# Attention scores as three f32r passes in a hybrid decoder block

## The chip, the cores and the metric

The kernel runs on one core of one Trainium2 chip. The metric is the device time of one execution in microseconds; runs of the kernel before took 970.04 to 971.68 us, with a median of 970.68 us over three runs. Everything is float32 data; products on TensorE are made either as float32 or as f32r, the chip's reduced float32 format, with values that were split into a high and a low part.

## The reference

A decoder block of one layer on 512 tokens of width 1024. Two branches share one input projection: a gated delta rule (8 heads of 128, in chunks) and a forgetting attention (8 heads of 128). Their outputs are merged by gates, and a squared-ReLU MLP of width 4096 follows. The part that the change touches is the attention:

```python
fqh = rmsnorm(to_heads(fq, FOX_HEADS), fox_q_norm_g[l])
fkh = rmsnorm(to_heads(fk, FOX_HEADS), fox_k_norm_g[l])
...
for i in range(t // FOX_BLOCK):            # 4 blocks of 128 queries
    q0 = i * FOX_BLOCK; q1 = q0 + FOX_BLOCK
    s = (einsum('bhqd,bhkd->bhqk', q[:, :, q0:q1], k[:, :, :q1]) * scale
         + cum[:, :, q0:q1, None] - cum[:, :, None, :q1])
    p = softmax(where(mask, s, -inf), axis=-1)
    outs.append(einsum('bhqk,bhkd->bhqd', p, v[:, :, :q1]))
```

So a head has four score products: 128 queries against 128, 256, 384 and 512 keys.

## The kernel before, in words

**Stages.** The kernel first normalises x and makes its high and low parts (`uhi`, `ulo`; to about 55 us). Then come the projections of the recurrence, `w_z` and `w_gdn`, by `dense` (L284): for each unit of weights, 8 contraction blocks with three f32r products of 512 columns (L290, L291, L294). The attention's q, k, v, the gates and later the projection of the attention's output come from `stream` (L959). It works by a scheme that replaces eight block products by seven (P1 to P7), with f32r products of 256 columns (L993), 24 for each unit. The merge (`w_pg`, by `dense`), `w_o` and the MLP (`w_u`, `w_d`; L1218 in the profile) end the kernel from about 609 us on.

**Weights.** Each weight tile arrives by DMA (`load`, L209), is copied to its high part by ScalarE (L271) and has its low part subtracted by VectorE (L272), two units ahead of the product (`prefetch_split`). In the MLP the same steps are L1462 and L1469.

**Side work.** Work that isn't the main sequence of weight products is written as Python generators, `tasks`. Each unit of the main sequence calls `tick()`, which lets every task go on to its next `yield`; I call that a round. The recurrence's heads (`head`), its inversion (`invert`, small VectorE steps L690 and L692), its scan over chunks and the attention (`fox_worker`) are such tasks. What a task writes in a round stands there in the program's order. The tile framework then plans: it simulates the program with its own estimates of durations and may reorder instructions on an engine; only the MLP's are in part kept in the order written.

**The attention.** Two `fox_worker` tasks take heads from the list `fq`, where `stream` puts each head once its q and k are there. A worker, per head: squares and a reciprocal root for the norms (L892 to L898), two empty rounds, then four transposes each of q and k into two PSUM banks `ptq` and `ptk` (L907, L908), copied to `qT` and `kT` by ScalarE with a scale (L911, L912). After a round, in each of six rounds, a stage of three query blocks: bias rows by ScalarE (L925, L926), the score product (L928), the sum with the bias and the row's extreme by VectorE (L931), the exponential by ScalarE (L933); one round later the reciprocal and the scaling (L940, L941) and the transposes of the probabilities (L944, copied in L946); one round later the product with v (L953). The head's output is copied (L956) and stored. While the second group of the recurrence is projected, `hold` keeps the workers from taking a further head.

**Buffers.** 53 pages of 128x512 float32 (`page`) are shared by nearly all of these; a page is free again when its last reader is done. Five PSUM banks with the tag "at" (`atps`) serve transposes, scores, scans and the rest; three serve the main sequence. ScalarE's functions stand in tables that have to be loaded (ACT_TABLE_LOAD): the exponential of L933, the sigmoid of L1095 and the SiLU of L611 and L1062 are not in one table here, as the loads in the profile show.

**After the attention.** `outputs_in` (L1091) waits until the recurrence, the workers and their stores are done and `stream` has begun its chunk 6; it applies the sigmoids to the gates (L1095) and splits the recurrence's outputs (rows read in L555, split in L301, L302). These feed the `w_pg` products of the merge.

Of the kernel before, what the change touches and what calls it, by code (L numbers as in the profile page):

```python
# [7 lines left out]
F32 = mybir.dt.float32  # L8
F32R = mybir.dt.float32r
AF = mybir.ActivationFunctionType  # L10
ALU = mybir.AluOpType
# [4 lines left out]
P = 128  # L16
# [28 lines left out]
def hybrid_block(tc, a, out):  # L45
# [21 lines left out]
    def nm(s):  # L67
        n_names[0] += 1
        return f"{s}_{n_names[0]}"
# [5 lines left out]
    def page(dt=F32, s="pg"):  # L75
        if s in FOX_TAGS:
            return fxp.tile([P, T], dt, tag=s, name=nm(s))
        tag = TAGS_OF.get(s, s)
        if tag in TAGS:
            return pgp.tile([P, T], dt, tag=tag, name=nm(s), bufs=TAGS[tag])  # L80
        return pgp.tile([P, T], dt, tag="pg", name=nm(s))
# [3 lines left out]
    def const(shape, s, dt=F32):  # L85
        return (cp if s in KEEP else cm).tile(shape, dt, tag=s, name=s)

    def small(n, s="sm"):
        return smp.tile([P, n], F32, tag="sm", name=nm(s))
# [12 lines left out]
    def atps(s="at"):  # L102
        return pat.tile([P, T], F32, tag="at", name=nm(s))

    def v3(ap, n):
        return ap.rearrange("p (a b) -> p a b", a=n)

    def bc(ap, n):
        return ap.unsqueeze(2).to_broadcast(list(ap.shape) + [n])

    def cs(c):
        return slice(c * P, (c + 1) * P)

    mm = nc.tensor.matmul
    vec, act, pool = nc.vector, nc.scalar, nc.gpsimd
# [23 lines left out]
    def start(gen):  # L139
        tasks.append(gen)  # L140
        return gen
# [3 lines left out]
    def store_late(dst, src):  # L145

        for _ in range(LATE):
            yield
        nc.sync.dma_start(dst, src)
# [172 lines left out]
    def small_in(name, shape, eng=None):  # L322
        t = const(shape, "c_" + name)
        (eng or nc.sync).dma_start(t, a[name])
        return t
# [19 lines left out]
    fk_g = small_in("fox_k_norm_g", [P, 1])  # L345
# [10 lines left out]
    fqs = const([P, 1], "fqs")  # L356
    pool.tensor_scalar(fqs, fq_g, float(P) ** -0.5, None, op0=ALU.mult)

    def rsq(dst, src):
        pool.tensor_tensor(dst, src, expo[:, 0:src.shape[-1]], op=ALU.pow)  # L360
# [501 lines left out]
    fq = []  # L862
# [6 lines left out]
    def bias_rows(n):  # L869

        if n < len(fq) and n not in rows_of:
            rows_of[n] = row_page(3, fq[n][0])
        return rows_of.get(n)

    def fox_worker(after=None):

        while after is not None and not inverted[after]:
            yield
        while taken[0] < H:
            if taken[0] >= len(fq) or hold[0]:  # L880
                yield
                continue
            h, qk, vt = fq[taken[0]]
            nr = bias_rows(taken[0])
            taken[0] += 1
            nd = page(s="nd")
            pool.affine_select(out=v3(nd[:, :], NCH), in_=v3(nr[:, :], NCH), compare_op=ALU.is_ge, fill=-1e30, base=0,
                               pattern=[[0, NCH], [-1, P]], channel_multiplier=1)
            sq = small(16, "fss")
            for half in range(2):  # L890
                junk = page(s="junk")
                act.activation(junk, qk[half], AF.Square)  # L892
                vec.tensor_reduce(sq[:, 4 * half:4 * half + 4], v3(junk[:, :], 4), axis=AX.X, op=ALU.add)
            vec.tensor_scalar(sq[:, 0:8], sq[:, 0:8], 1.0 / P, EPS, op0=ALU.mult, op1=ALU.add)
            rsq(sq[:, 8:16], sq[:, 0:8])
            for half in range(2):
                t = v3(qk[half][:, :], 4)
                pool.tensor_tensor(t, t, bc(sq[:, 8 + 4 * half:12 + 4 * half], P), op=ALU.mult)  # L898
            yield
            yield  # L900
            bias_rows(taken[0])
            ptq = atps("fqT")
            ptk = atps("fkT")
            for tb in range(NCH):
                t = qk[tb // 2]
                i = tb % 2
                nc.tensor.transpose(ptq[:, cs(tb)], t[:, cs(2 * i)], ident)  # L907
                nc.tensor.transpose(ptk[:, cs(tb)], t[:, cs(2 * i + 1)], ident)  # L908
            qT = page(s="fq")
            kT = page(s="fk")  # L910
            act.activation(qT, ptq, AF.Copy, scale=fqs)  # L911
            act.activation(kT, ptk, AF.Copy, scale=fk_g)  # L912
            yield
            while not vt:
                yield
            po = None
            st = {}
            for step in range(NCH + 2):
                i = step
                if i < NCH:  # L920
                    n = (i + 1) * P
                    s = cs(i)
                    bias = page(s="bias")
                    if i:
                        act.activation(bias[:, :n - P], nr[:, :n - P], AF.Identity, bias=cc[:, i, h:h + 1])  # L925
                    act.activation(bias[:, s], nd[:, s], AF.Identity, bias=cc[:, i, h:h + 1])  # L926
                    psc = atps("sc")
                    mm(psc[:, :n], qT[:, s], kT[:, :n], start=True, stop=True)  # L928
                    sm = small(4, "fsm")
                    pt = page(s="p")  # L930
                    vec.tensor_tensor_reduce(out=pt[:, :n], in0=psc[:, :n], in1=bias[:, :n], scale=-1.0,  # L931
                                             scalar=3.0e38, op0=ALU.add, op1=ALU.min, accum_out=sm[:, 0:1])
                    act.activation(pt[:, :n], pt[:, :n], AF.Exp, bias=sm[:, 0:1], scale=-1.0,  # L933
                                   accum_out=sm[:, 1:2])
                    st[i] = [pt, sm]
                i = step - 1
                if 0 <= i < NCH:
                    n = (i + 1) * P
                    pt, sm = st[i]
                    vec.reciprocal(sm[:, 2:3], sm[:, 1:2])  # L940
                    vec.tensor_scalar(pt[:, :n], pt[:, :n], sm[:, 2:3], None, op0=ALU.mult)  # L941
                    pT = atps("pT")
                    for c in range(i + 1):
                        nc.tensor.transpose(pT[:, cs(c)], pt[:, cs(c)], ident)  # L944
                    pTs = page(s="pTs")
                    act.copy(pTs[:, :n], pT[:, :n])  # L946
                    st[i] = pTs
                i = step - 2
                if 0 <= i < NCH:
                    if po is None:  # L950
                        po = atps("fo")
                    for c in range(i + 1):
                        mm(po[:, cs(i)], vt[c], st[i][:, cs(c)], start=(c == 0), stop=(c == i))  # L953
                yield
            o = page(s="ob")
            act.copy(o, po)  # L956
            stores.append(start(store_late(obd[:, h].rearrange("i p t -> p i t"), v3(o[:, :], 2))))
# [110 lines left out]
    box = {}  # L1068
    start(decays(0, box, gt))
    fws = [start(fox_worker()) for _ in range(NFW)]  # L1070
    fu = []
    ch0 = gdn_group(0, box, {1: lambda: fu.append(start(factors_u()))})
# [377 lines left out]
    for k, (w, c, p, s_) in enumerate(MLP):  # L1450
# [6 lines left out]
        n = pos[0]  # L1457
        pos[0] += 1
        new = range(len(units), min(len(seq), n + 1 + LA_MLP))
        for m in new:  # L1460
            hi, lo = whl.tile([P, D], F32R, tag="hi", name=nm("hi")), whl.tile([P, D], F32R, tag="lo", name=nm("lo"))
# [5 lines left out]
        for m in new:  # L1467
            hi, lo = units[m]
# [108 lines left out]
```

## Time and profile before

| | |
|---|---|
| median of 3 runs | 970.68 us (970.04 to 971.68) |
| profiled execution | 970.2 us, span 968.4 us |
| TensorE busy (PE) | 957.4 us, 99% |
| weight loads (PEld) | 868.9 us, 90% |
| VectorE busy (DVE) | 743.1 us, 77% |
| ScalarE busy (ACT) | 646.4 us, 67% |
| GpSimd busy (POOL) | 217.4 us, 22% |
| granted TensorE clock | 1.000 of full speed |

How to read it: the span is the time from the first to the last instruction. A matmul's end is modelled, and matmuls overlap, so PE at 99% says that TensorE nearly always had work in flight and not that each instruction was as short as it could be. PEld is the loading of the stationary operand, which runs beside the products. "Idle before" in a group's row is the idle time of that engine just ahead of its instructions, with the instruction that ended it. The chain that ended last is followed back from the last instruction; its pieces are start and length in microseconds, engine, tile and line.

### The profile page before, as it was taken

To read this page: it belongs to the slowest core of one execution; us is meant where nothing else is said; L and a number is where in the kernel's file an instruction comes from. 1 tells how busy PE (TensorE), PEld (TensorE's weight loads), DVE (VectorE), ACT (ScalarE), POOL (GpSimd) and SP (SyncE) were. 2 spreads that over 40 slices of the span, in tenths; PEclk is the share of its full clock that TensorE was granted. 3 is DMA by queue.
4 is the path that set the end of the run, shared out by engine and by line. 5 is a ranking of instruction groups with operands and counts; after the bars stand their busy time and mean duration, and the time that the engine had idled before them with its cause. 6 is when DMAs were issued, how large, how long until landed. Compare 5 with 4: busy or idle time off the path is not lost.

```text
span 968.4 us, 17456 instructions
## 1 busy us (share of the span) xinstructions
PE 957.4 (99%) x6610; PEld 868.9 (90%) x6610; DVE 743.1 (77%) x1249; ACT 646.4 (67%) x1096; POOL 217.4 (22%) x224
## 2 busy tenths in 40 slices
PE   9999999999999999999999999999999999999998
PEld 6788889998888999989999899889989989988986
DVE  6877979956478799665656887979886796697696
ACT  7879755778575767889556454678755755666761
POOL 1503222340343243322220110202122021121110
PEclk9999999999999999999999999999999999999999
DMA  8457679755677877657689687878798788888883
GB/s 288 138 156 240 187 181 204 170 147 165 207 235 185 195 179 150 153 143 195 189 178 319 153 221 204 156 184 171 173 213 180 197 165 202 182 176 197 191 168 113
DMA packets 87291, 180.38 MB, mean 186 GB/s; under 512 B 8152, under 2 KB 41048, under 8 KB 87208
## 3 DMA queue, kind: packets, MB, share of 16 engines
q0 software_dynamic: 17392, 63.12, 37.6%
q1 hardware_dynamic: 69816, 116.15, 37.4%
q8 instruction: 52, 0.85, 0.3%
q14 instruction: 31, 0.25, 0.1%
HBM read 160.11 MB, written 19.14 MB: 185 GB/s over the span
## 4 chain that ended last, share of the span: by engine, by line
PE 93%; ACT 4%; DVE 1%; issue 1%; DMA 1%; SPq 0%; ACTq 0%; DVEq 0%
PE mlp L1218 36%; PE st L993 23%; PE mm L294 7%; PE mm L290 7%; PE mm L291 7%; PE fo L953 2%; PE sc L928 2%; PE pT L944 1%; PE v L804 1%; PE kk L649 1%; PE kq L657 1%; PE o L825 1%; PE o L824 1%; ACT hi L271 1%; DMA x<-xT 1%
## 5 line engine op out<-in xcount | busy, mean ns | idle before, releaser
L1462 ACT CAST hi<-draw 128x1024 fp32r<-128x1024 f32 x124 | 129.9, 1049 | 116.8 <-PE mlp L1218 101.2
L1469 DVE TENSOR_TENSOR lo<-draw,hi 128x1024 fp32r<-128x1024 f32 x124 | 151.3, 1222 | 45.9 <-ACT hi L1462 42.7
L271 ACT CAST hi<-sraw 128x1024 fp32r<-128x1024 f32 x84 | 87.9, 1048 | 83.9 <-PE st L993 49.0
L272 DVE TENSOR_TENSOR lo<-sraw,hi 128x1024 fp32r<-128x1024 f32 x84 | 105.5, 1257 | 26.1 <-ACT hi L271 20.9
L1218 PE MATMUL mlp<-hi,shi 128*128 128x512 f32 x280 | 109.4, 391 | 0.7 <-ACT hi L1462 0.6
L1218 PE MATMUL mlp<-hi,slo 128*128 128x512 f32 x280 | 109.1, 390 | 0.0
L1218 PE MATMUL mlp<-lo,shi 128*128 128x512 f32 x280 | 109.0, 389 | 0.0
L1218 PE MATMUL mlp<-shi,hi 128*128 128x256 f32 x448 | 90.3, 283 | 0.0
L1218 PE MATMUL mlp<-slo,hi 128*128 128x256 f32 x448 | 90.3, 283 | 0.0
L1218 PE MATMUL mlp<-shi,lo 128*128 128x256 f32 x448 | 90.3, 283 | 0.0
L291 PE MATMUL mm<-ulo,hi 128*128 128x512 f32 x216 | 84.8, 395 | 1.3 <-DVE ulo L305 1.3
L290 PE MATMUL mm<-uhi,hi 128*128 128x512 f32 x216 | 84.8, 396 | 0.1
L232 POOL DMA_DIRECT2D sraw<-w_st x36 | 31.6, 878 | 190.1 <-DVE lo L272 141.2
L993 PE MATMUL st<-lo,hi 128*128 128x256 f32 x432 | 73.9, 287 | 0.0
L993 PE MATMUL st<-hi,lo 128*128 128x256 f32 x432 | 72.2, 285 | 0.0
L993 PE MATMUL st<-hi,hi 128*128 128x256 f32 x432 | 71.7, 287 | 0.0
L1218 PEld LDWEIGHTS mlp<-shi,hi 128*128 128x128 f32 x448 | 70.6, 192 | 0.9
L1218 PEld LDWEIGHTS mlp<-shi,lo 128*128 128x128 f32 x448 | 69.9, 192 | 0.0
L1218 PEld LDWEIGHTS mlp<-slo,hi 128*128 128x128 f32 x448 | 69.8, 192 | 0.0
L272 DVE TENSOR_TENSOR lo<-raw,hi 128x1024 fp32r<-128x1024 f32 (+1 forms) x42 | 50.1, 1197 | 22.0 <-ACT hi L271 16.1
L1218 PEld LDWEIGHTS mlp<-hi,shi 128*128 128x128 f32 x280 | 52.6, 188 | 11.9 <-ACT hi L1462 0.8
L1218 PEld LDWEIGHTS mlp<-lo,shi 128*128 128x128 f32 x280 | 52.6, 188 | 11.0
(343 smaller groups left out, 2314.2 us busy)
## 6 DMA issues: line engine op xcount, KB each, us to landing
sraw<-w_st POOLq DMA_DIRECT2D x36, 512.0 KB, 6.1
draw<-w_u POOLq DMA_DIRECT2D x32, 512.0 KB, 6.1
draw<-w_d POOLq DMA_DIRECT2D x32, 512.0 KB, 6.9
sraw<-w_st SPq DMA_DIRECT2D x27, 512.0 KB, 5.1
draw<-w_d SPq DMA_DIRECT2D x26, 512.0 KB, 4.4
raw<-w_gdn SPq DMA_DIRECT2D x24, 512.0 KB, 4.0
draw<-w_u SPq DMA_DIRECT2D x24, 512.0 KB, 4.5
hd<-hd SPq DMA_DIRECT2D x34, 256.0 KB, 4.1
```

The lines of the kernel that those rows point to most:

```text
L232: nc.gpsimd.dma_start(raw, a[w][c, q, s_], accum_op=ALU.add)
L271: act.copy(hi[:, c], raw[:, c])
L272: vec.tensor_tensor(lo[:, c], raw[:, c], hi[:, c].bitcast(F32), op=ALU.subtract)
L290: mm(o, w, rhi(k), start=(k == 0), stop=False)
L291: mm(o, w, rlo(k), start=False, stop=False)
L294: mm(o, lo[:, k * cols:(k + 1) * cols], rhi(k), start=False, stop=(k == KT - 1))
L928: mm(psc[:, :n], qT[:, s], kT[:, :n], start=True, stop=True)
L953: mm(po[:, cs(i)], vt[c], st[i][:, cs(c)], start=(c == 0), stop=(c == i))
L993: mm(o, u, w, start=first and t == 0 and k == 0 and j == 0 and x is hi, stop=x is lo and k == 3, skip_group_check=True)
L1218: return (lambda *args, **kw: tc.keep_in_program_order(f(*args, **kw))) if self.pinned[0] else f
L1462: pact.copy(hi, raws[m][0])
L1469: pvec.tensor_tensor(lo, raws[m][0], hi[:, :].bitcast(F32), op=ALU.subtract)
```

## The change

The transposed q and k of a head are written as f32r high parts (`qT`, `kT`, by ScalarE as before), and VectorE makes f32r low parts (`ql`, `kl`) by scaling the transposes once more and subtracting the high parts. The score products of query blocks 1, 2 and 3 (256, 384 and 512 keys) become three f32r passes that add up in PSUM: high by high, high q by low k, low q by high k. Block 0 (128 keys) keeps a float32 product; its operands are made by VectorE in a further page, `qk0`. A further `yield` stands before the scores.

```diff
-            qT = page(s="fq")
-            kT = page(s="fk")
+            qk0 = page(s="qk0")
+            qT, ql, kT, kl = [page(F32R, "fqk") for _ in range(4)]
             act.activation(qT, ptq, AF.Copy, scale=fqs)
             act.activation(kT, ptk, AF.Copy, scale=fk_g)
+            for x, src, by in ((qk0[:, 0:P], ptq, fqs), (qk0[:, P:2 * P], ptk, fk_g)):
+                vec.tensor_scalar(x, src[:, 0:P], by, None, op0=ALU.mult)
+            for hi, lo, src, by in ((qT, ql, ptq, fqs), (kT, kl, ptk, fk_g)):
+                vec.scalar_tensor_tensor(lo, src, by, hi[:, :].bitcast(F32), op0=ALU.mult, op1=ALU.subtract)
+            yield
             yield
             while not vt:
                 yield
...
                     psc = atps("sc")
-                    mm(psc[:, :n], qT[:, s], kT[:, :n], start=True, stop=True)
+                    if i:
+                        mm(psc[:, :n], qT[:, s], kT[:, :n], start=True, stop=False)
+                        mm(psc[:, :n], qT[:, s], kl[:, :n], start=False, stop=False)
+                        mm(psc[:, :n], ql[:, s], kT[:, :n], start=False, stop=True)
+                    else:
+                        mm(psc[:, :n], qk0[:, 0:P], qk0[:, P:2 * P], start=True, stop=True)
```

## The prediction, made before the changed kernel ran

> **What bounds the kernel now.** I read the page's totals, then the chain that ended last, then the busy time by stretches, then the single groups.
>
> ```profile
> span 968.4 us, 17456 instructions
> PE 957.4 (99%) x6610; PEld 868.9 (90%) x6610; DVE 743.1 (77%) x1249; ACT 646.4 (67%) x1096; POOL 217.4 (22%) x224
> PE 93%; ACT 4%; DVE 1%; issue 1%; DMA 1%; SPq 0%; ACTq 0%; DVEq 0%
> PE mlp L1218 36%; PE st L993 23%; PE mm L294 7%; PE mm L290 7%; PE mm L291 7%; PE fo L953 2%; PE sc L928 2%; PE pT L944 1%; PE v L804 1%; PE kk L649 1%; PE kq L657 1%; PE o L825 1%; PE o L824 1%; ACT hi L271 1%; DMA x<-xT 1%
> ```
>
> TensorE carries 93% of the chain, and the scores of L928 stand in it with 2%. Matmul durations overlap, so I take the price of a product from the chain, where a piece lasts until the next one starts. By stretches (columns: length, then busy time and count for PE, PEld, DVE, ACT, POOL):
>
> ```profile
> 140.00:360.00 220.00, 220.00 (x1724) 202.61 (x1723) 166.71 (x367) 153.10 (x310) 68.29 (x64) 1.00 0.73 187
> 360.00:395.00 35.00, 35.00 (x287) 34.10 (x286) 34.14 (x86) 24.41 (x45) 15.06 (x15) 1.00 0.69 166
> 395.00:410.00 15.00, 15.00 (x120) 14.05 (x120) 9.23 (x19) 12.75 (x26) 2.64 (x3) 1.00 0.71 143
> 410.00:470.00 60.00, 58.09 (x631) 54.53 (x630) 35.36 (x79) 50.38 (x90) 14.48 (x13) 1.00 0.67 180
> ```
>
> ```profile
> L956 ACT COPY ob<-fo x8: 566/587/607, 203.5 to 464.9; 128x512 f32<-128x512 f32 x8
> L911 ACT ACTIVATE fq<-fqT,fqs x8: 670/689/694, 177.7 to 434.9; 128x512 f32<-128x512 f32 x8
> ```
>
> The attention heads run from 177.7 us (the copy of the first transposed q) to 464.9 (the start of the last head's output copy). There TensorE has no hole before 410 us and loses 1.91 us of 60 after it, so a shorter score product should shorten the span. Two other things matter. VectorE is busy 34.14 of 35 us in 360 to 395. And in 402 to 433 us the chain leaves TensorE several times for ScalarE:
>
> ```profile
> 402.44 0.61 ACT X L708
> 408.35 1.28 ACT L1095
> 410.29 1.28 ACT L933
> 412.99 1.88 ACT hi L271 x2
> 428.98 1.28 ACT L1095
> 430.92 1.28 ACT L933
> ```
>
> L1095 and L933 at 1.28 us are table loads: sigmoids of the gates and exponentials of the attention take turns there.
>
> **The change, part by part.**
>
> *Score products of 256, 384 and 512 keys.* One float32 product is two instructions; the new form is three. What they cost in the chain (start, length, what):
>
> ```profile
> 179.70 0.66 PE sc L928 x4
> 185.98 0.65 PE sc L928 x2
> 189.35 0.22 PE fo L953 x2
> 189.57 0.86 PE sc L928 x2
> 180.36 5.51 PE st L993 x46
> 525.47 1.86 PE mm L294 x8
> ```
>
> The first row holds the calls of 128 and 256 keys together. A float32 product of 128 columns is 0.22 us (the fo row), which leaves 0.44 for 256 keys; 384 take 0.65, 512 take 0.86. An f32r instruction of 256 columns takes 5.51/46 = 0.120 us, one of 512 takes 1.86/8 = 0.2325. For 384 I interpolate: 0.176. Three passes are then 0.36, 0.53 and 0.70 us, against 0.44, 0.65 and 0.86. Saved: 0.08 + 0.12 + 0.16 = 0.36 us a head, for 8 heads 2.9 us. If 384 columns cost as much as 512, it would be 0.17 a head less, 1.5 us in all; if all three sizes ran without the fixed part (0.2325/512 = 0.454 ns a column), 0.349, 0.523 and 0.697, 0.38 a head, 3.1 us. I take 2.9.
>
> The Trainium skill ("TensorE: Matmul & The Clock Gate", section "Back-to-back issue gap") puts a lone stream at N/2.4 + 2.5 ns: 216 ns for 512, 109 for 256. By it the estimate would be 1.46 us for the nine passes and a saving near 3.9 us; the trace, at 232 and 120 ns with a weight load beside each instruction, is above it.
>
> *128 keys.* The product stays float32 and its duration stays 0.22 us. Its operands now come from VectorE, by two multiplications of 128 columns out of PSUM.
>
> *VectorE.* Added per head: those two, and two scalar_tensor_tensor of 128x512 that read PSUM and SBUF. Nearest rows:
>
> ```profile
> L931 DVE CUSTOM_DVE_ANT_0 p<-sc,bias 128x128 f32<-128x128 f32 x8 | 2.3, 286 | 1.5 <-PE sc L928 1.5
> L783 DVE SCALAR_TENSOR_TENSOR zc<-omT,c_gdn_norm_g,zc x8: 739/744/751, 256.6 to 500.6; 128x512 f32<-128x512 f32 x8
> L272 DVE TENSOR_TENSOR lo<-sraw,hi 128x1024 fp32r<-128x1024 f32 x84 | 105.5, 1257 | 26.1 <-ACT hi L271 20.9 <-PE st L993 2.9 <-PE mm L294 2.0
> L911 ACT ACTIVATE fq<-fqT,fqs x1: 689/689/689, 363.2 to 363.2; 128x512 f32<-128x512 f32 x1
> L911 ACT ACTIVATE fq<-fqT,fqs x1: 689/689/689, 390.3 to 390.3; 128x512 f32<-128x512 f32 x1
> ```
>
> 2 x 0.286 + 2 x 0.744 = 2.06 us a head, 16.5 us in all. VectorE idles 53 us in 140 to 360, 5.8 in 395 to 410 and 24.6 in 410 to 470, which covers six heads. It idles only 0.9 us in 360 to 395, where two heads are transposed (the last two rows, at 363 and 390 us): 4.1 us of work, of which 3.2 spill past 395. What runs there beside the weight splits (1.257 us each) is the inversion chain of the second recurrence group, which gives way; so the splits should stay on time. Lower bound 0; upper bound: the 3.2 us land whole on TensorE. If the cover were gone everywhere, all 16.5 us would show; the idle time above excludes that.
>
> *ScalarE.* The two copies of L911 and L912 write f32r instead of float32:
>
> ```profile
> L304 ACT ACTIVATE uhi<-x,c_norm_mix_g 128x512 fp32r<-128x512 f32 x8 | 5.7, 709 | 0.0
> L912 ACT ACTIVATE fk<-fkT,c_fox_k_norm_g 128x512 f32<-128x512 f32 x8 | 5.4, 681 | 0.0
> ```
>
> At most 0.05 us a head (L911's median is 689 ns), 0.4 in all, hidden except for the two heads at 401 and 435 us, where the chain is on ScalarE: 0.1 us.
>
> *New waits.* The score of 256 keys now waits for the subtractions on VectorE, after the copies on ScalarE; behind it in TensorE's order wait stream products L993, if the planner has put them there. The wait grows by up to 2.06 us of VectorE work plus its queue. The two PSUM banks of the transposes (of the five with the tag "at") are read for that much longer: up to 2 us for 2 banks, 8 times. Who needs a bank then are the later score and transpose products. The planner that orders instructions when the kernel is built knows these dependencies and can put a stream product (2.87 us for 24 instructions) between; below nothing this cannot be, and above I take 1 us at each of the two heads transposed at 401 and 435 us, where ScalarE is on the chain: 2 us.
>
> *Pages.* A head holds five pages (qk0, qT, ql, kT, kl) in place of two, out of 53. No row counts pages; the nearest sign is that the row inputs, the first of them read at 372 us, are split only at 510, as if for want of pages. Price: 0 to one unit of the stream, 2.87 us.
>
> *The extra round.* Each head takes ten rounds of the main loop instead of nine. In the code the last head is then taken at entry 24 of STREAM instead of 23 and ends two rounds later, 34 instead of 32; the branch's outputs are waited for at entry 40. In time: the last head's copy is at 464.9 us, the splits of the row inputs follow at 510, so 45 us cover some 6 us. No head moves across the pause that `hold` makes: head 2 is taken one round later, head 3 after the pause as before. Price nothing.
>
> *A new order.* Twelve instructions a head more or changed make the planner's estimates different from the first head on. What order can do is seen in the holes that TensorE has now: 1.91 us in 410 to 470, and after the heads
>
> ```profile
> 609.00:660.00 51.00, 50.28 (x277) 43.21 (x276) 44.89 (x61) 38.23 (x68) 7.77 (x9) 1.00 0.81 174
> 660.00:968.00 308.00, 304.28 (x1937) 277.48 (x1935) 242.81 (x288) 189.66 (x254) 52.74 (x61) 1.00 0.82 180
> 964.32 0.75 DVE acc L1346
> ```
>
> 0.72 us; the 3.72 us after 660 are the end, where the last sum starts at 964.32 and only stores follow. So between a gain of 2.6 us and a loss of as much; middle zero.
>
> *Sum.* -2.9 for the products, +0.1 ScalarE, +0.3 for the late waits of both kinds (bounds 0 and 3.2 + 2; nearest row 360 to 395, where TensorE has no hole although VectorE is full): -2.5 us. The profiled execution took 970.2 us (span 968.4 and 1.8 around it), 0.5 below the median of 970.68. It becomes 967.7, and the median 968.2. A measurement of this kernel tells about 0.2%, 1.9 us, from no change: faster means below 968.7, slower above 972.6.
>
> **The rivals.**
>
> *The gain is given back at the merge.* The first products of w_pg need the recurrence's rows:
>
> ```profile
> L555 SPq DMA_DIRECT2D row<-oad x8: 319/324/443, 372.2 to 515.8; - x8
> 517.74 0.23 PE mm L290
> 519.50 0.62 ACT L301 CAST hi<-row 128x512 fp32r<-128x512 f32 x1 [0.62 <-DMA row<-oad]
> 519.82 2.07 DVE L302 TENSOR_TENSOR lo<-row,hi 128x512 fp32r<-128x512 f32 x3
> 525.23 0.24 PE mm L291
> ```
>
> The last split ends at 521.9, the last product that needs it starts at 525.2: 3.3 us of slack. If TensorE comes 2.9 us earlier and the inversion chain 3.2 us later, 2.8 us are missing and the time is 970.6, no change. For it: ScalarE already waited 0.62 us there for the load. Against it: the row splits wait for more than the recurrence (its last output, L783, is at 500.6), so they may move up with TensorE.
>
> *The tables alternate more.* This is the one that ends slower. The place is 402 to 465 us, where sigmoids of the gates and exponentials of the last three heads share ScalarE:
>
> ```profile
> L933 ACT ACT_TABLE_LOAD x8 | 10.3, 1283 | 1.0 <-DVE fsm L931 0.9
> L1095 ACT ACT_TABLE_LOAD x5 | 6.4, 1283 | 0.1
> L1095 ACT ACTIVATE gate<-gate 128x512 f32<-128x512 f32 x8 | 5.1, 632 | 0.5 <-DVE gate L971 0.4
> ```
>
> A head whose exponentials come 2 to 6 us later meets more sigmoids. Each further pair of loads costs 2.57 us of ScalarE in a stretch where the chain runs over it (ScalarE 50.38 of 60 busy). It decides from two pairs on: 5.1 against the 2.5 saved and the 1.9 of the bound. With two pairs the time is 973.3. For it: there are 8 sigmoids and only 5 loads, so three more can come. Against it: TensorE lost only 1.91 us after 410, although the loads at 410, 429 and 431 us above lie there.
>
> *The weight loads bind, not the columns.* Three instructions need three loads where two needed two. Then a call gains nothing from fewer cycles and pays one more load, 0.11 us by the fo row (0.22 for two loads and two products of 128 columns): 24 x 0.11 = 2.6 us slower, 973.3. Against it: 0.86 us for two instructions of 512 columns is far above two loads, and 256 and 512 columns differ by 0.11 us, which loads would not. The Trainium skill ("Perfetto Trace Analysis", section "Identifying the Most-Contended Engine") asks to judge TensorE by the busy share of its weight loads rather than of its products; here that share is 90%, so by this rule loads would come first. The chain's rows speak against it, and it gets little.
>
> **How the numbers follow.** The forecast (gain of 1.9 us or more reaches the end) 0.51; given back at the merge or by the late waits, within the bound, 0.28; the tables or the pages cost more than the gain, slower, 0.18; loads bind 0.03. So faster 0.51, same 0.28, slower 0.21. Within the forecast the range is 965.2 (3.1 saved and a better order, 2.4) to 968.7. To leave out no more than 2 in 10 the range takes in no change and the slower case with two pairs: 965.2 to 973.3. The predicted time is that of the forecast, 968.2.
>
> **What would show it.** Right: three rows for the f32r score with 0.12, 0.17 and 0.23 us an instruction in the chain; four new VectorE groups of 0.29 and 0.75 us, 16 to 17 us in all; VectorE near full in 360 to 400 and TensorE without new holes. The recurrence's last output near 500 us and w_pg 2 to 3 us earlier than 517.7. Wrong: holes of TensorE before scores that wait for VectorE, more than 5 loads at L1095, ScalarE or TensorE waiting at the merge for row loads, or passes that take as long as the product they replace. The prediction fails above all if the planner's new order moves work of other branches by more than the 2.9 us at stake.

## The result, and the profile after

The changed kernel takes 967.97 us (median of 7 runs, 966.91 to 968.34), the kernel before beside it on the same chip 971.13 (970.04 to 972.66): a ratio of 0.997, 95% interval 0.9961 to 0.9979, or 2.9 us less by the ratio (2.0 to 3.8; the medians differ by 3.2). The forecast was 968.2 us and 2.5 less. The profiled execution took 968.33 us, 1.9 less than the profiled one of before; the one run of the seven without the halved clock told of below took 966.91.

The head of the page of the changed kernel (lines below the scores have numbers higher by 10: L933 is now L943, L956 is L966, L993 is L1003, L1095 is L1105, L1218 is L1228):

```profile
span 966.5 us, 17529 instructions
PE 956.0 (99%) x6634; PEld 873.6 (90%) x6634; DVE 756.2 (78%) x1281; ACT 645.0 (67%) x1096; POOL 219.7 (23%) x224
```

The scores in the chain of work, for one head (start, length, what; L934 to L936 are the three passes):

```profile
448.72 0.12 PE sc L934
448.84 0.12 PE sc L935
448.96 0.12 PE sc L936
...
452.96 0.17 PE sc L934
453.13 0.18 PE sc L935
453.31 0.18 PE sc L936
...
459.47 0.23 PE sc L934
459.70 0.23 PE sc L935
459.94 0.23 PE sc L936
```

0.36, 0.53 and 0.69 us for 256, 384 and 512 keys: the forecast had 0.36, 0.53 and 0.70. The groups of the added VectorE work, and ScalarE's first copy (durations are least/median/most in ns, then first and last start):

```profile
L914 DVE TENSOR_SCALAR qk<-fqT,fqs x8: 339/348/353, 179.4 to 437.4; 128x128 f32<-128x128 f32 x8
L914 DVE TENSOR_SCALAR qk<-fkT,c_fox_k_norm_g x8: 342/344/345, 180.3 to 438.3; 128x128 f32<-128x128 f32 x8
L916 DVE SCALAR_TENSOR_TENSOR fqk<-fkT,c_fox_k_norm_g,fqk x8: 740/744/744, 180.5 to 438.6; 128x512 fp32r<-128x512 f32 x8
L911 ACT ACTIVATE fqk<-fqT,fqs x8: 681/689/692, 177.9 to 436.7; 128x512 fp32r<-128x512 f32 x8
```

The same stretches as before (length, then busy time and count of PE, PEld, DVE, ACT, POOL, then granted clock, DMA share, GB/s):

```profile
140.00:360.00 220.00, 219.35 (x1733) 204.37 (x1732) 175.07 (x382) 151.86 (x309) 69.86 (x66) 1.00 0.72 186
360.00:395.00 35.00, 35.00 (x293) 34.81 (x293) 34.41 (x85) 24.56 (x45) 13.60 (x12) 1.00 0.76 174
395.00:410.00 15.00, 15.00 (x125) 14.84 (x125) 14.21 (x35) 14.07 (x28) 3.16 (x4) 1.00 0.80 182
410.00:470.00 60.00, 59.46 (x649) 58.03 (x648) 36.00 (x83) 49.82 (x90) 16.19 (x14) 0.97 0.72 180
```

VectorE's spill past 395 us is there (9.23 us busy before, 14.21 now), and TensorE has no hole from it. In 410 to 470 TensorE idles 0.54 us instead of 1.91. New is the clock of 0.97. The same view by single microseconds:

```profile
419.00:420.00 1.00, 1.00 (x6) 1.00 (x6) 0.97 (x2) 1.00 (x4) 0.00 (x0) 0.52 0.11 41
420.00:421.00 1.00, 1.00 (x7) 1.00 (x6) 0.68 (x3) 0.97 (x3) 0.00 (x0) 0.50 0.63 70
421.00:422.00 1.00, 1.00 (x7) 1.00 (x7) 0.00 (x0) 0.22 (x1) 0.00 (x0) 0.50 0.76 303
422.00:423.00 1.00, 1.00 (x7) 1.00 (x7) 0.00 (x0) 0.00 (x0) 0.00 (x0) 0.78 0.95 354
```

For about 3.4 us the clock is granted at half: 0.48 + 0.50 + 0.50 + 0.22 = 1.7 us of full-speed work lost. From the merge (516 us) to the end nothing else differs. The first product of the MLP's `w_u` comes 1.9 us earlier, as much as the span shrank (the first row below is of the kernel before, the second of the changed one), and what follows it lasts 319.0 to 319.4 us in every kernel of this study:

```profile
L1218 PE MATMUL mlp<-shi,hi x448: 277/283/364, 649.4 to 920.0; 128*128 128x256 f32 x150
```

```profile
L1228 PE MATMUL mlp<-shi,hi x448: 277/283/364, 647.5 to 918.1; 128*128 128x256 f32 x150
```

So every kernel can be accounted for by the time of this product, called the start of the MLP from here on. I divided that time from the trace: each TensorE product counts by how far its end moves TensorE's last end, the time in between is idle, and the loss to the clock is the time at half clock times one half. The parts add up to the start of the MLP within 0.2 us.

| kernel | profiled run | MLP starts | scores, 256 to 512 keys | all other products, at full clock | idle | lost to clock |
|---|---|---|---|---|---|---|
| before | 970.2 | 649.4 | 16.1 | 626.6 | 6.9 | 0 |
| changed | 968.3 | 647.5 | 12.8 | 626.8 | 6.4 | 1.7 |
| e1, float32 scores | 970.3 | 649.0 | 15.9 | 627.4 | 5.9 | 0 |
| e2, passes alone | 970.8 | 649.6 | 13.1 | 628.2 | 8.5 | 0 |
| e3, no extra round | 973.9 | 652.7 | 13.0 | 628.6 | 11.3 | 0 |
| e4, one pass | 968.8 | 648.0 | 4.8 | 627.8 | 10.4 | 5.1 |
| e5, round in before | 968.2 | 647.3 | 15.7 | 624.8 | 6.9 | 0 |
| e6, one more round | 975.0 | 654.1 | 12.9 | 626.0 | 12.0 | 3.4 |
| e7, split inversion | 979.1 | 658.0 | 13.3 | 627.1 | 12.7 | 5.1 |
| e8, double VectorE work | 973.7 | 652.5 | 13.3 | 627.0 | 10.6 | 1.7 |
| x1, float32, order of changed | 969.7 | 648.4 | 15.7 | 626.3 | 6.6 | 0 |
| x2, passes, order of before | 969.1 | 648.3 | 13.3 | 626.2 | 7.3 | 1.7 |
| x3, passes, order of e5 | 967.7 | 646.8 | 13.0 | 624.9 | 9.1 | 0 |
| x4, change, order of e5 | 977.9 | 657.1 | 13.1 | 624.3 | 14.7 | 5.1 |

Each row is one execution, and the last column isn't a fixed property of a kernel. Beside the experiments, 22 of 56 executions of the kernel before also had a mean clock of 0.998 or less; they took 971.8 us in the median, the others 970.2. Of the changed kernel 6 of 7 had. Where in the kernel the clock was low is known for the profiled executions only. Two further executions of the kernel before, at clocks of 0.85 and 0.785, took 1043 and 1737 us and are left out of these counts and of the ratios.

### The profile page after: what moved, and what is told of

It is laid out like the page before. It is cut to its first block, busy times and chain, and to the rows that moved or that the text cites. A ratio compares the mean times of both kernels' runs of the same rounds, so it can differ in the third digit from the quotient of the medians.

```text
span 966.5 us, 17529 instructions
## 1 busy us (share of the span) xinstructions
PE 956.0 (99%) x6634; PEld 873.6 (90%) x6634; DVE 756.2 (78%) x1281; ACT 645.0 (67%) x1096; POOL 219.7 (23%) x224
## 4 chain that ended last, share of the span: by engine, by line
PE 71%; DVE 3%; issue 2%; ACT 2%; DMA 1%; POOL 0%; POOLq 0%; DVEq 0%
PE mlp L1228 36%; PE st L1003 14%; PE mm L290 4%; PE mm L291 4%; PE mm L294 4%; PE fo L963 1%; DMA sraw<-w_st 1%; DVE lo L272 1%; PE o L825 1%; PE v L804 1%; PE w L796 1%; PE o L824 1%; PE S L813 1%; PE pT L954 1%; PE T L749 0%
## 5 line engine op out<-in xcount | busy, mean ns | idle before, releaser
L271 ACT CAST hi<-sraw 128x1024 fp32r<-128x1024 f32 x84 | 88.1, 1049 | 78.4 <-PE st L1003 44.2
L1228 PE MATMUL mlp<-hi,shi 128*128 128x512 f32 x280 | 109.4, 391 | 0.7 <-ACT hi L1472 0.6
L1228 PE MATMUL mlp<-hi,slo 128*128 128x512 f32 x280 | 109.1, 390 | 0.0
L1228 PE MATMUL mlp<-lo,shi 128*128 128x512 f32 x280 | 109.0, 389 | 0.0
L1228 PE MATMUL mlp<-slo,hi 128*128 128x256 f32 x448 | 90.3, 283 | 0.0
L1228 PE MATMUL mlp<-shi,lo 128*128 128x256 f32 x448 | 90.3, 283 | 0.0
L1228 PE MATMUL mlp<-shi,hi 128*128 128x256 f32 x448 | 90.3, 283 | 0.0
L1003 PE MATMUL st<-hi,hi 128*128 128x256 f32 x432 | 73.1, 288 | 0.0
L1003 PE MATMUL st<-hi,lo 128*128 128x256 f32 x432 | 71.6, 284 | 0.0
L1228 PEld LDWEIGHTS mlp<-shi,hi 128*128 128x128 f32 x448 | 70.6, 192 | 0.9
L1003 PE MATMUL st<-lo,hi 128*128 128x256 f32 x432 | 71.3, 285 | 0.0
L1228 PEld LDWEIGHTS mlp<-shi,lo 128*128 128x128 f32 x448 | 69.9, 192 | 0.0
L1228 PEld LDWEIGHTS mlp<-slo,hi 128*128 128x128 f32 x448 | 69.8, 192 | 0.0
L1228 PEld LDWEIGHTS mlp<-hi,shi 128*128 128x128 f32 x280 | 52.6, 188 | 11.8 <-ACT hi L1472 0.8
L1228 PEld LDWEIGHTS mlp<-lo,shi 128*128 128x128 f32 x280 | 52.6, 188 | 11.0
```

Of the source, the lines that this page charges most:

```text
L271: act.copy(hi[:, c], raw[:, c])
L1003: mm(o, u, w, start=first and t == 0 and k == 0 and j == 0 and x is hi, stop=x is lo and k == 3, skip_group_check=True)
L1228: return (lambda *args, **kw: tc.keep_in_program_order(f(*args, **kw))) if self.pinned[0] else f
```

## The experiments

### One part at a time, in the order that the planner then writes

The first four kernels start from the changed one; the kernel before took 970.5 us beside them.

**e1: float32 scores, all else as changed.**

```diff
-                        mm(psc[:, :n], qT[:, s], kT[:, :n], start=True, stop=False)
-                        mm(psc[:, :n], qT[:, s], kl[:, :n], start=False, stop=False)
-                        mm(psc[:, :n], ql[:, s], kT[:, :n], start=False, stop=True)
+                        mm(psc[:, :n], qT[:, s].bitcast(F32), kT[:, :n].bitcast(F32), start=True, stop=True)
```

> The changed kernel with its two low parts, its extra page and its extra round, but with the scores of blocks 1 to 3 as one float32 product of the high parts read as float32, so the low parts are made and not used. Theory (the gain is TensorE's, 2.9 us of score passes, and the side work is hidden): the gain is gone, 970.9 us, within 1.0 of the kernel before (971.1). Rival A (the planner's new order and the fewer holes of TensorE make the gain, the passes nothing): it stays near the changed kernel, 968.0, at most 969. Rival B (the side work costs something that the passes paid for): above 972.1.

970.13 us, ratio 0.9992 (0.9984 to 1.0). The gain is gone, as the theory had it. But the table shows that the order of the other work moved too: TensorE's idle and its other products are not those of the changed kernel.

**e2: the passes alone.**

```diff
-            qk0 = page(s="qk0")
-            qT, ql, kT, kl = [page(F32R, "fqk") for _ in range(4)]
+            qT, kT = [page(F32R, "fqk") for _ in range(2)]
...
-            for x, src, by in ((qk0[:, 0:P], ptq, fqs), (qk0[:, P:2 * P], ptk, fk_g)):
-                vec.tensor_scalar(x, src[:, 0:P], by, None, op0=ALU.mult)
-            for hi, lo, src, by in ((qT, ql, ptq, fqs), (kT, kl, ptk, fk_g)):
-                vec.scalar_tensor_tensor(lo, src, by, hi[:, :].bitcast(F32), op0=ALU.mult, op1=ALU.subtract)
-            yield
...
-                        mm(psc[:, :n], qT[:, s], kl[:, :n], start=False, stop=False)
-                        mm(psc[:, :n], ql[:, s], kT[:, :n], start=False, stop=True)
+                        mm(psc[:, :n], qT[:, s], kT[:, :n], start=False, stop=False)
+                        mm(psc[:, :n], qT[:, s], kT[:, :n], start=False, stop=True)
...
-                        mm(psc[:, :n], qk0[:, 0:P], qk0[:, P:2 * P], start=True, stop=True)
+                        mm(psc[:, :n], qT[:, s].bitcast(F32), kT[:, :n].bitcast(F32), start=True, stop=True)
```

> The three f32r passes without the work that feeds them: no low parts, no extra page, no extra round; all three passes of blocks 1 to 3 multiply the high parts, block 0 the high parts read as float32, so the low parts are left out. Theory (VectorE's 16.7 us and the three pages are hidden): within 1.2 us of the changed kernel, 967 to 969; the 1.2 is what its halved TensorE clock near 420 us costs, if that goes away here. Rival (the side work on VectorE, the banks and the pages cost TensorE 2 us or more): 966 or less.

970.63 us, ratio 1.0 (0.9989 to 1.0012): a miss for the theory and for the rival. The scores are 3.0 us shorter in the table, and 1.6 us more idle and 1.6 us more in other products eat it. Without any added VectorE work, without a page more and without the round, the passes gain nothing in the order that the planner wrote for them.

**e3: the change without its further round.**

```diff
                 vec.scalar_tensor_tensor(lo, src, by, hi[:, :].bitcast(F32), op0=ALU.mult, op1=ALU.subtract)
-            yield
             yield
```

> The changed kernel without the extra round between the low parts and the first score. Theory (the round only moves a head's work within the planner's freedom): within 1.0 us of the changed kernel, 967 to 969. Rival (the round is what keeps TensorE from waiting for the low parts): 970 or more, with named waits of TensorE for VectorE at the scores.

975.5 us, ratio 1.0047 (1.0032 to 1.0061), another miss: one `yield` is worth 7.5 us. The time is the rival's, but the rival's wait isn't there, as the rows show. (The profiled execution, 973.94 us at a clock of 0.999, is the fastest of six; the other five, at 0.995 to 0.998, took 974.86 to 976.37.) Its stretch from 410 to 470, its chain there, and two rows of what TensorE waited for from 140 to 470 (us in total, times, longest):

```profile
410.00:470.00 60.00, 56.02 (x622) 53.27 (x621) 37.41 (x80) 52.23 (x92) 12.74 (x12) 1.00 0.62 161
```

```profile
411.93 1.28 ACT L942
...
414.27 0.50 DVE p L950
...
414.82 0.67 PE pT L953 x4
415.49 0.59 ACT AT L722
...
416.73 0.61 ACT AT L722
...
417.35 0.61 ACT AT L722
...
417.99 1.04 ACT hi L271
419.04 0.86 ACT pTs L955 x2
419.90 0.39 ACT p L942 x2
```

```profile
PE pT L953 <- DVE p L950: 2.4, 4, 0.8
...
PE sc L937 <- DVE qk L914: 0.4, 1, 0.4
```

This is the place at which the prediction had found the chain on ScalarE. The inversion's copies (L722), a weight split (L271), an exponential's table load (L942) and a head's probabilities stand behind one another there, and TensorE idles 4.0 us. What it waits for are mostly probabilities; for the change's added VectorE work it waits 0.4 us (the last row).

**e4: one pass in place of three.**

```diff
-                        mm(psc[:, :n], qT[:, s], kT[:, :n], start=True, stop=False)
-                        mm(psc[:, :n], qT[:, s], kl[:, :n], start=False, stop=False)
-                        mm(psc[:, :n], ql[:, s], kT[:, :n], start=False, stop=True)
+                        mm(psc[:, :n], qT[:, s], kT[:, :n], start=True, stop=True)
```

> The changed kernel with one f32r pass for blocks 1 to 3 instead of three (high parts only; the two passes with low parts are left out). Theory (each pass lies on the chain at 0.12, 0.175 and 0.23 us): 8 x 2 x 0.525 = 8.4 us less than the changed kernel, 959.6, within 1.5. Rival (the heads' stretch is bound by VectorE and ScalarE, TensorE only fills): at most 3 us less, 965 or more.

968.01 us, ratio 0.9971 (0.9959 to 0.9983). It takes 8.0 us more out of the scores than the change does and ends no sooner: 4.0 us come back as idle, 3.4 as half clock, 1.0 in other products. The theory is missed by 8 us and the time is the rival's; since the order changed as well, the rival's reason isn't shown by it.

### The order by itself

Beside these the kernel before took 970.28 us.

**e5: the kernel before with the further round, and nothing else.**

```diff
             act.activation(kT, ptk, AF.Copy, scale=fk_g)
+            yield
             yield
```

> The kernel before with nothing but the extra round put in ahead of the scores: the same instructions, another order. First theory (a round moves nothing that counts): 970.5 within 1.0. Second theory, formed after the first four runs (any edit makes the planner write another order, and the order alone moves the time by some us through holes of TensorE between 190 and 460 us and through its halved clock after them): it differs from 970.5 by more than 1 us, either way, and the difference is found in those holes and in the clock.

968.22 us, ratio 0.9974 (0.9963 to 0.9984). The second theory had the size right, but not the place. By the medians the empty round gives nearly as much as the whole change; all seven of its executions had a clock of 0.999 or more, and the one of the changed kernel that had (966.91 us) is 1.3 us faster than its median. Idle is the same in sum: the 1.91 us that the kernel before lost in 410 to 470 are gone (below), but 1.6 appear between 205 and 410. What falls is the other products, by 1.7 us: the inversion's products of 32x32 (L717, L730), which follow one another with shorter waits in this order, take 1.8 us less by this count.

```profile
410.00:470.00 60.00, 60.00 (x663) 57.34 (x662) 36.53 (x80) 47.84 (x88) 15.67 (x15) 1.00 0.73 182
```

**e6: one `yield` more than the change has, two more than the kernel before.** 

```diff
             yield
             yield
+            yield
```

> The changed kernel with two rounds more ahead of the scores: the same instructions, another order. If the extra round helps because low parts are ready when TensorE comes to the scores: as the changed kernel, 968.0 within 1.0, since they are ready with one round already. If order alone moves the time (second theory): it differs by more than 1 us, and the holes and the clock account for it.

975.0 us, ratio 1.0046 (1.0028 to 1.0064). So a round isn't a gain as such; 5.6 us of idle and 1.7 of clock are added to those of the changed kernel (its profiled execution lost the clock in the first 15 us, far from the scores).

**e7: a pause in the inversion's second loop**, which was to part the 32x32 products that precede the half clock.

```diff
         for i in range(NI):
+            if i == NI // 2:
+                yield
             s = slice(i * B, (i + 1) * B)
```

> The changed kernel with a round in the middle of the second loop of 32x32 products of the inversion, so that stream products can stand between. Theory on the clock (the halving near 420 us follows a stretch of small products with holes): the clock is 1.000 and the time 1 to 2 us below the changed kernel, 966.5. Rival (the halving follows the holes alone, or the new order brings other holes): no gain, 968 or more, and a clock below 1 where holes come before it.

981.61 us, ratio 1.011 (1.0097 to 1.0124). This is the rival's case. The half clock came for three times as long in all instead of going: for 6.8 us from 325.6 us on, while a hole of 5.0 us stood open at a product that waits for `conv` (L609, the recurrence), and for 3.4 us at 428.0, behind the small products.

**e8: the added VectorE work twice.** 

```diff
             for x, src, by in ((qk0[:, 0:P], ptq, fqs), (qk0[:, P:2 * P], ptk, fk_g)):
                 vec.tensor_scalar(x, src[:, 0:P], by, None, op0=ALU.mult)
+            for x, src, by in ((qk0[:, 0:P], ptq, fqs), (qk0[:, P:2 * P], ptk, fk_g)):
+                vec.tensor_scalar(x, src[:, 0:P], by, None, op0=ALU.mult)
+            for hi, lo, src, by in ((qT, ql, ptq, fqs), (kT, kl, ptk, fk_g)):
+                vec.scalar_tensor_tensor(lo, src, by, hi[:, :].bitcast(F32), op0=ALU.mult, op1=ALU.subtract)
             for hi, lo, src, by in ((qT, ql, ptq, fqs), (kT, kl, ptk, fk_g)):
                 vec.scalar_tensor_tensor(lo, src, by, hi[:, :].bitcast(F32), op0=ALU.mult, op1=ALU.subtract)
```

> The changed kernel with the four new VectorE instructions of a head issued twice, 17 us more of VectorE work. Theory (VectorE is covered by its idle time outside 360 to 395 us): at most 1.5 us above the changed kernel, 969.5. Rival (VectorE's load between 360 and 410 us reaches TensorE): 3 us or more above, 971 or more, with TensorE waiting for VectorE there. Order alone can move it as well, so the verdict rests on what TensorE waits for.

973.73 us, ratio 1.0032 (1.002 to 1.0044). 17 us more on VectorE cost 5.8 us against the changed kernel. The MLP starts 5.0 us later, and idle grows by 4.2. At the scores TensorE waits only 0.3 us for this work; stream products wait 2.1 us for the copies and sums of the stream's own results in `fqk` (ScalarE and VectorE). The time is the rival's, the wait only in part. The work itself and the order that it brings can't be told apart here.

### The order held fixed

All of these change the order, so a part's own price can't be read from them. In the last four kernels each instruction is tied to the one that it follows in another kernel's plan, engine by engine:

```diff
         hybrid_block(tc, aps, out)
+        pin(tc, list(nc.cur_bb.bb.instructions))
...
+    for a, b in zip(order, order[1:]):
+        tc.add_manual_dep(mine[b], mine[a].name, nosync, reason="pinned order")
```

The second part is the core of `pin`: `mine` are an engine's instructions as the program writes them, `order` is their order in the other kernel's plan (lists of numbers). In the traces of x1, x2 and x3 the instructions other than scores stand in the other kernel's order, but for 4 of 6546 on TensorE in x2. No kernel was tied to its own plan, so it isn't measured by itself whether the ties cost anything. The kernel before took 970.97 us beside these.

**x1: e1's program in the order of the changed kernel.**

> The changed kernel with one float32 product of the high parts (the low parts are made but not used) in place of the three passes, and with the order of every engine's instructions fixed to the one that the changed kernel has: only the score products differ. Theory (the passes save what their own rows show, 2.9 us by the forecast, about 3.5 by the busy time of the score groups, and the planner's order does the rest): 2.9 to 3.5 us slower than the changed kernel, 970.9 to 971.5; if the halved clock near 419 us (1.7 us) does not come, 969.2 to 969.8. Rival (the gain of the change came from the order, and a shorter score product is lost in waits): within 0.7 us of the changed kernel, 967.3 to 968.7.

969.55 us, ratio 0.9983 (0.9974 to 0.9992); the granted clock is 1.00. This is the branch of the theory without the half clock. In the rows for the head shown above the float32 scores stand with 0.43, 0.64 and 0.86 us:

```profile
449.26 0.43 PE sc L934 x2
453.56 0.64 PE sc L934 x2
460.19 0.86 PE sc L934 x2
```

From x1 to the changed kernel the scores lose 2.9 us (15.73 to 12.84), and 1.7 of these are taken by the half clock. And x1, with float32 scores and all the added work, is 1.7 us faster than the kernel before (0.8 to 2.5 by the interval). Not all of this is the order's. Fewer executions of x1 met the half clock (2 of 12, against 6 of 16 of the kernel before); at a clock of 0.999 or more the medians are 969.51 and 970.46, and in the profiled executions the MLP starts 1.0 us earlier. So the order, with the added work in it, is worth about 1.0 us.

**x2: e2's program in the order of the kernel before.**

> The kernel before with three f32r passes of the high parts alone for blocks 1 to 3 (low parts left out, block 0 one float32 product), no extra round, and every engine's order fixed to that of the kernel before. Theory (own price of the passes): 2.9 to 3.5 us faster than the kernel before, 967.0 to 967.6 for 970.5, with no more holes than before (6.9 us ahead of the MLP). Rival (order made the gain): within 0.7 us of the kernel before, 969.8 to 971.2. The same passes in the planner's own order took 970.63.

967.9 us, ratio 0.9966 (0.9952 to 0.9979), or 3.3 us less by the ratio, as the theory had it; at a clock of 0.999 or more the medians are 967.58 and 970.46, 2.9 us apart. The scores lose 2.9 us (16.12 to 13.25); idle grows by 0.4. The same program in its own order (e2) gained nothing. Its profiled execution met the half clock in the first 13 us, far from the scores, and took 969.09.

**x3: the passes of high parts in the order of e5.**

> The kernel before with only the extra round took 968.22. Here it has three f32r passes of the high parts for blocks 1 to 3 as well (low parts left out), with every engine's order fixed to that of the kernel with only the extra round. Theory (passes and order add up): 968.2 less 2.9 to 3.5, 964.7 to 965.3. Rival (both gains are the same slack, taken once): 967.5 to 968.5.

967.42 us, ratio 0.9963 (0.995 to 0.9976), against e5's 0.9974: the time is close to the rival's range and far from the theory's. The intervals overlap, so that the two gains add up isn't shown. The scores lose 2.7 us and idle gains 2.2, most of it in one piece of the chain:

```profile
418.16 0.18 PE sc L929
418.34 1.55 issue
419.89 0.33 PE sc L930
```

TensorE stands still between the first and the second pass of one score and waits for nothing that the profile shows. What it is stays open.

**x4: the whole change with TensorE, ScalarE, GpSimd and SyncE in the order of e5**, VectorE's order being the planner's.

> The whole change, with its low parts and all of VectorE's added work, with TensorE, ScalarE, GpSimd and SyncE in the order of the kernel before with only the extra round; VectorE's order is the planner's. Theory (passes and order add up, the added VectorE work is hidden): 964.7 to 966.0, below both kernels. Rival (the VectorE work delays the scores where TensorE's order leaves no room for it): holes of TensorE ahead of scores and probabilities, 967.5 to 971.

978.52 us, ratio 1.0072 (1.0059 to 1.0085): the rival's case, and worse than it said. The chain shows how:

```profile
404.79 0.27 DVE qk L914
405.06 0.66 DVE fqk L916
405.72 0.26 DVE qk L914
405.98 0.66 DVE fqk L916
406.63 1.07 DVE Xd L698
...
409.35 0.62 DVE XT L701
...
409.99 0.62 ACT AT L722
...
411.88 0.61 ACT AT L722
...
412.49 1.28 ACT L1105
...
414.32 0.36 ACT pTs L956
...
414.73 1.23 PE fo L963 x4
```

```profile
PE fo L963 <- ACT pTs L956: 3.9, 1, 3.9
```

The 1.85 us of added VectorE work stand ahead of the inversion (L698, L701), the inversion's copies on ScalarE wait for it, and a table load and `pTs` stand behind the copies; in a fixed order TensorE waits 3.9 us for it, and the half clock follows for some 10 us (5.1 lost). The order of e5 was good for a program without this work.

## Why the prediction came out right, and which step of it failed

**The passes: right.** 2.9 us was forecast from the chain's rows. With the order held, the scores of 256 to 512 keys lose 2.89 us (x1 to changed) and 2.87 us (before to x2); 384 columns, which were interpolated, take 0.175 us. At full clock before and x2 lie as far apart in time, 2.9 us. The rival that weight loads bind is refuted by the three rows of the passes: three loads each, and a time that goes with the columns. The share by which the Trainium skill has TensorE judged ("Perfetto Trace Analysis", section "Identifying the Most-Contended Engine"), that of the weight loads, couldn't tell this here: it is 90% before and after, and the loads' busy time even rose (868.9 to 873.6 us) in the faster kernel.

**VectorE: nearly right.** Twice 0.345 and twice 0.743 us make 2.18 us a head instead of 2.06, 17.4 us in all. The spill lies where it was put, past 395 us, and costs no hole in this order. x4 shows that the work can reach TensorE when the order leaves no room: one wait of 3.9 us, above the bound of 3.2.

**ScalarE's f32r output: nothing** instead of 0.1 (689 ns before and after). **Late waits**: idle is 0.5 us less than before, not 0.3 more.

**The rivals.** The merge gives nothing back: the first `w_pg` product in the chain starts at 515.86 instead of 517.74.

```profile
515.86 0.23 PE mm L290
```

The recurrence's last output starts at 498.6 instead of 500.6. The tables alternate as often as before:

```profile
L943 ACT ACT_TABLE_LOAD x8 | 10.3, 1283 | 0.1
L1105 ACT ACT_TABLE_LOAD x5 | 6.4, 1283 | 0.1
```

**The steps that failed are "A new order" and "The extra round".** The one was priced at zero between a gain of 2.6 us and a loss of as much, the other at nothing. The bounds came from the holes that TensorE had, but a new order can make holes where there were none, and the clock can halve behind them. The prediction named an order that moves other branches' work as what would make it fail above all. (The lower end of its range, 965.2, counts 2.4 us of gain from the order where its own part has 2.6; with 2.6 it is 965.0.) Measured: the round alone takes 2.1 us off the kernel before (e5), its absence costs the changed kernel 7.5 (e3), a second one 7.0 (e6). The order of the changed kernel by itself is worth about 1.0 us (x1 against before, at full clock), inside the bounds; e3, e6, e7 and x4, which all have the passes, end 4.7 to 11.3 us above the kernel before.

So the passes gave what was forecast, and that the whole sum came out is in part luck. The order took about 1.0 us off; the half clock, which costs 1.7 us and came in 6 of 7 executions of the changed kernel against 22 of 56 of the kernel before, gave part of it back. Neither was forecast, and the 0.4 us put on for ScalarE and late waits didn't come. What stays open: which feature of an order decides, beyond the place (402 to 425 us, where inversion, exponentials, sigmoids and weight splits share ScalarE); whether pages ever bind, which wasn't tried; and whether a version with both e5's order and the passes can be had. No kernel with the whole computation was faster than the changed one.

## What to carry to other kernels

Read the price of a shorter instruction from the chain, but before crediting it with the time measured, hold the order fixed: where a planner rewrites the program at each edit, the same instructions in another order took from 2 us less (e5, against the kernel before) to 14 us more (e7, against the changed kernel), and an empty `yield` gained nearly as much as the change did. An engine at 99% is no promise: with 11.3 us less score work on TensorE, the kernel ended only 2.5 us sooner (e4). Look for the stretch where a second engine feeds the full one, and at the granted clock of every execution, since one half-clock window cost 1.7 us here, more than half of what the passes save.

## What the runs showed of the hardware

- **The half clock without a long hole.** In the changed kernel the longest hole ahead of the halving is 0.54 us, up to 416.2 us, behind which 96 products of 32x32 follow until 418.7; the clock halves at 419.0 for 3.4 us. In the other kernels it lasted 3.4, 6.8 or 10.2 us, so in steps of 3.4. The Trainium skill ("TensorE: Matmul & The Clock Gate", section "What's actually happening") has the half rate, a free-running window of about 3.4 us, and that it varies between runs; these runs agree (one run of the changed kernel in seven went without it). Its section "HAM oscillation — how this bites in real kernels" puts the cause, in the case that it tells, in idle gaps above about 3.4 us; holes of 5.0 us (e7) and 3.9 us (x4) did stand ahead of a halving here, but so did 0.54 us with the small products behind. Neither was enough alone: the profiled execution of x1, in the same order, with the same 96 products and no hole of more than 0.02 us ahead of them from 410 us on, kept the full clock, and so did the profiled execution of e3, whose holes in 410 to 470 come to 4.0 us, the longest 1.2.
- **What the halvings have in common.** In every trace the clock changes at whole multiples of 3.413 us after it first became full, which marks off fixed stretches. Of such a stretch (3.413 us), TensorE spent 0.55 us on products larger than 32x32 in the one ahead of the changed kernel's halving (415.6 to 419.0 us), and 0.72 (x4), 0.92 and 1.06 (e7), 1.09 (e8) and 1.26 (e4) in those ahead of the others between 60 us and the MLP. Of the 2421 stretches there in all traces, only two more have less than 1.41: e7's at 325.6, already at half clock, which went on, and x1's at 417.7 (1.08), whose clock stayed full. So the halving seems to go by how little TensorE does in one fixed stretch, and where the stretches fall differs between executions. This was counted in the traces afterwards; no kernel was made to test it.
- **A multiplication of 128 columns out of PSUM** takes VectorE 0.345 us (mean of the 16 of L914); the estimate from the row of L931 was 0.286.
